# A hybrid decoder trunk on one core: tables and half gates in the first stage, rotary in place, norm gains in the weights

## The chip, the core and the metric

The kernel runs on one core of a Trainium2 chip. The engines are TensorE (PE in the profile, with its weight loads as PEld), VectorE (DVE), ScalarE (ACT), GpSimd (POOL) and SyncE (SP, which here only issues DMAs). The metric is the device time of one execution in microseconds; the median of several runs counts.

## The reference

Two layers run on a sequence of 1024 tokens with 1024 features. Each layer modulates a normalised input by a condition vector c, projects it once, runs three groups of heads, and projects back:

```python
mod = c_act @ w_mod + b_mod                      # c_act = silu(c)
shift, scale, gate = split(mod, 3)
h = rms_norm(x, pre_gain) * (1 + scale) + shift
aq, ak, av, ag, rq, rk, rv, rg, gq, gk, gv, gg, ga = split(h @ w_in)
a_out = window_attention(rotary(aq), rotary(ak), av, sinks) * silu(ag)
r_out = rms_norm(retention(rotary(rq), rotary(rk), rv)) * silu(rg)
g_out = rms_norm(gla(gq, gk, gv, gates(ga)), gla_norm_gain) * silu(gg)
y = concat(a_out, r_out, g_out) @ w_out
x = x + gate * rms_norm(y, post_gain)
```

The rotary angles are position times frequency, one set of 32 frequencies for attention and one for retention; their sines and cosines are made on the chip and are used by both layers. The gain `gla_norm_gain` has 64 entries per layer, the same for all four heads of the third group.

## The kernel before

**Tiles.** The tokens are 8 tiles of 128, in 4 pairs; features are 8 blocks of 128 (KT = 8). The modulated input of a pair is kept transposed, as a high part in the reduced format that TensorE reads and a low part that is the remainder (`hi`, `lo`). Weights are split the same way. A projection of one tile, `project`, is 24 matmuls: three products (high and high, high and low, low and high) for each of 8 blocks. The helper at L161 records almost every matmul, L176 every transpose, L145 many copies on ACT, L150 most DMAs, so these lines stand for many places in the code.

**Weights.** `load` brings one 256-column unit of w_in or w_out in four pieces of 256 KB. The high part is made by ACT (L473) or DVE (L475), the low part by POOL or DVE (L478). The unit of the third group's gate, gg, has 272 columns: 256 of gate and 16 of the low-rank `ga` (L484, L485).

**Buffers.** Four rings of on-chip buffers matter: t2 (512 columns, 10 of them), t1 (256 columns, 8), the PSUM banks `mm` (3) for projections and `aux` for transposes and small results. `mix_tile` gives two large tiles, which hold x of tiles 2 and 3 first, the zeroed operands of the third group later and mixed rows after that.

**Order of work.** The code records the work in an order; a scheduling layer then lays out each engine's instructions and may set one ahead of others recorded earlier. Long steps are generators (`job`), which yield a due time, and `pump` runs those whose time has come by a clock in the code that adds up a cost for each matmul. The due times stand in the table L (pf3, gz1, tt1 and so on). The assignment of operations to engines stands in the table EN. `issue_after` keeps an instruction behind a given one in that layer. Engines take their instructions in order.

**The first stage.** `mod_first` makes shift and gain of layer 0 in two halves (hh = 0, 1) of 512 columns each. The weight tiles `wm` land in pieces on SP's queue. For each of 8 blocks PE multiplies c_act with the shift columns (one row, `pm`), and DVE accumulates the gain columns in `acc` (L322, L324). After a half, ACT copies the row out, and `finish` turns both into columns with 16 tiny matmuls and three small operations on DVE (L304 to L306). The finish of the first half is placed behind the second block of the second half (FIN = 1). Meanwhile x of tiles 0 and 1 is normalised: ACT squares (L530), DVE and POOL make the factor (L513, L514, L519), DVE scales (L545), and PE transposes. Modulation (L577 on ACT, L579 on DVE), the high part (L583, ACT) and the low part (L566, L587) follow. Tiles 2 and 3 come after the first stage (`soon`), tiles 4 to 7 as jobs of `pre_first`.

**After it.** The gates gg and rg of each pair of tiles are projected (`do_gates`), with `silu2` (L861, L863) on each. For gg, `gla_logits` multiplies the silu with the norm gain `gn5` (L872) and stores it to sgS. The sine tables (`tables`, L411 to L439) run as a job from 70 to 93 us in the profile, next to the gates of later tiles, and `tables_T` transposes them. Then the decays of the third group (L918 to L943) and the retention queries rq, with `rotary` (L698 to L704), which reads PSUM three times per tile; each tile of rq holds one of the three `mm` buffers until its third read.

**Small loads.** Constants, the sinks, `gwt` and `gn5` are loaded on SP's queue. The retention gate is stored to srS and loaded again later; those loads are on ACT's queue, other loads on SP's.

Of the kernel before, what the change touches and what calls it, by code (L numbers as in the profile page):

```python
# [89 lines left out]
def trunk(ctx: ExitStack, tc: tile.TileContext, ins, cst, out):  # L90
# [168 lines left out]

    modc = {}  # L260
# [28 lines left out]
    def mod_first(rws, between):  # L289
# [6 lines left out]
        def finish(hh, row, acc):  # L296
            pc = mm()
# [11 lines left out]
        late = None  # L309
        for hh in range(2):  # L310
# [9 lines left out]
            for k in range(KT):  # L320
                if k == 0:
                    V.tensor_scalar(acc, wm[1][:, k], c_act[:, k:k + 1], None, ALU.mult)  # L322
                else:
                    mark[2] = V.scalar_tensor_tensor(acc, wm[1][:, k], c_act[:, k:k + 1], acc, ALU.mult, ALU.add)  # L324
# [3 lines left out]
                if late is not None and k == FIN:  # L328
                    pump()
                    finish(0, *late)  # L330
                    pump()
# [5 lines left out]
        pump()  # L337

    def mod_third(l, j):
# [9 lines left out]
        for hh in range(2):  # L349
            c0 = j * D + 512 * hh  # L350
            acc = gp.tile([P, 512], F32, tag="acc", name=nm("acc"), bufs=1)
            if j == 2:
                G.memset(acc, 0.0)
                nc.sync.dma_start(acc[0:1, :], b_mod[l:l + 1, c0:c0 + 512])
# [44 lines left out]

    MAGIC = 1.5 * 2.0 ** 23  # L400
# [7 lines left out]
    def tables():  # L408
        PIF = float(np.nextafter(np.float32(math.pi), np.float32(0)))
        ang = t2()  # L410
# [3 lines left out]
        nn = t2()  # L414
# [7 lines left out]
        n2 = t2()  # L422
# [4 lines left out]
        red = t2()  # L427
# [4 lines left out]
        yield  # L432
# [5 lines left out]
        yield  # L438
        V.tensor_scalar(cs, cs, 1.0, None, ALU.add)  # L439
# [17 lines left out]

    def unit(l, name):
        return place(PLACE[l][name])

    def load(l, name, first=None):
# [6 lines left out]
        for kc in range(KT // 2):  # L468
# [3 lines left out]
            if first == 0:  # L472
                A.activation(hi, st, AF.Copy)  # L473
            elif first == 1:
                V.tensor_copy(hi, st)  # L475
            else:
                copy(f"whi{kc}", hi, st)
            (G if first == 0 else eng(f"wlo{kc}")).tensor_tensor(wt[:, 1, 2 * kc:2 * kc + 2, 0:256], st, f(hi), ALU.subtract)  # L478
# [32 lines left out]
    def rstd_of(ss, w, scale, eps):  # L511
        r = small(w)
        V.tensor_scalar(r, ss, scale, eps, ALU.mult, ALU.add)  # L513
        G.tensor_tensor(r, r, mhalf[:, :w], ALU.pow)  # L514
# [9 lines left out]
    mark = [None] * 4  # L524
    eb = []

    def squares(xt, to):
        ss = small(2)
        for j in range(2):
            A.activation(to[j], xt[j], AF.Square, accum_out=ss[:, j:j + 1])  # L530
        return ss

    def pre(l, t, xt, early=False, soon=False):
# [7 lines left out]
        for j in range(2):  # L541
            if EN[f"xn{j}"] == "A":
                A.activation(xn[j], xt[j], AF.Copy, scale=r)
            else:
                V.tensor_scalar(xn[j], xt[j], r, None, ALU.mult)  # L545
        yield 0.5 if early else L["pf1"] if soon else lat("pre1", l)


        at = {}

        def turn(kt, bank, i):
            at[kt] = bank[:, i * P:(i + 1) * P]
            transp(at[kt], xn[kt // 4][:, kt % 4 * P:(kt % 4 + 1) * P], ident)

        if early:
            if not eb:
                eb.extend((aux(), aux()))
            x = aux()
            for kt in range(KT):
                turn(kt, x if kt < 4 else eb[kt // 6], kt if kt < 4 else 2 * t + kt % 2)  # L560
        late = []
        for j in range(2):
            yield (0.0, ("modh", l, j))
            if late:
                with tc.issue_after(mark[2].ins):
                    V.tensor_tensor(*late.pop(), ALU.subtract)  # L566
            if not early:
                x = aux()
                for k in range(4):
                    turn(4 * j + k, x, k)  # L570
            hf = t2()
            for k in range(4):
                kt = 4 * j + k
                ks = slice(k * P, (k + 1) * P)
                gain, shift = modc[(l, 1)][:, kt:kt + 1], modc[(l, 0)][:, kt:kt + 1]
                if kt < 6 if early else EN[f"mod{j}"] == "A":
                    A.activation(hf[:, ks], at[kt], AF.Identity, scale=gain, bias=shift)  # L577
                else:
                    mark[3] = V.tensor_scalar(hf[:, ks], at[kt], gain, shift, ALU.mult, ALU.add)  # L579
# [3 lines left out]
            mark[0] = A.activation(hi, hv, AF.Copy)  # L583
            if early and j == 0:
                late.append((lo, hv, f(hi)))
            else:
                i = (V if early else eng(f"hlo{j}")).tensor_tensor(lo, hv, f(hi), ALU.subtract)  # L587
                if early:
                    mark[1] = i
# [5 lines left out]

    def pre_first(t):
# [4 lines left out]

    def mix_tile(dt=F32R):
        return gp.tile([P, 2, KT, P], dt, tag="mx", name=nm("mx"), bufs=2)
# [10 lines left out]

    def between(hh, k):
        if hh == 0 and k == -1:
            load(0, "gg", 0)
        elif hh == 0 and k == 3:
            for t in range(2):
                job(pre(0, t, xe[t], True))  # L620
            pump()
        elif hh == 0 and k == 5:
            clk[0] += 0.6
            pump()
        elif hh == 1 and k == -1:
            for t in (2, 3):
                load_x(t, xe[t], nc.sync)

# [4 lines left out]
    with tc.issue_after(mark[0].ins), tc.issue_after(mark[3].ins):  # L633
        for t in (2, 3):
            job(pre(0, t, xe[t], soon=True))
        pump()
    with tc.issue_after(mark[0].ins), tc.issue_after(mark[1].ins):
        load(0, "rg", 1)
    for t in range(4, NT):
# [719 lines left out]
```

## Time and profile before

| | us |
|---|---|
| Median of 3 runs | 1026.69 (1024.07 to 1027.69) |
| The profiled execution | 1029.65 |
| Its span, first to last instruction | 1027.9 |
| TensorE busy | 989.8 (96%) |
| VectorE, ScalarE, GpSimd busy | 652.7, 388.3, 282.3 |
| Mean granted TensorE clock | 0.981 |
| HBM traffic | 137.1 MB, 133 GB/s over the span |

The profiled execution is one of the fast kind and 2.96 us above the median. Busy times are sums over the whole span; a stage that matters little in them can still set the end. A row of the timeline has the start, the duration, engine and line, what is written and read, the number of instructions merged into it and, in brackets, how long the engine had stood idle before and what released it.

### The profile page before, as it was taken

To read this page: it belongs to the slowest core of one execution; us is meant where nothing else is said; L and a number is where in the kernel's file an instruction comes from. 1 tells how busy PE (TensorE), PEld (TensorE's weight loads), DVE (VectorE), ACT (ScalarE), POOL (GpSimd) and SP (SyncE) were. 2 spreads that over 40 slices of the span, in tenths; PEclk is the share of its full clock that TensorE was granted. 3 is DMA by queue.
4 is the path that set the end of the run, shared out by engine and by line. 5 is a ranking of instruction groups with operands and counts; after the bars stand their busy time and mean duration, and the time that the engine had idled before them with its cause. 6 is when DMAs were issued, how large, how long until landed. Compare 5 with 4: busy or idle time off the path is not lost.

```text
span 1027.9 us, 19498 instructions
## 1 busy us (share of the span) xinstructions
PE 989.8 (96%) x7185; PEld 844.1 (82%) x7185; DVE 652.7 (63%) x1583; ACT 388.3 (38%) x1112; POOL 282.3 (27%) x310
## 2 busy tenths in 40 slices
PE   6899999899999999999999999999999999999997
PEld 2699899889898777777889999988899877777886
DVE  3789756857557687664578296585676477663322
ACT  2476221323222555642554242123332256553111
POOL 2332100424231244431235020133233134532000
PEclk8899999999899999999999999999999999999999
DMA  9742513523225344677545151243132323436753
GB/s 327 270 132 68 170 52 93 162 78 105 91 78 175 93 130 138 220 245 239 180 148 181 47 153 59 84 115 116 35 102 78 113 81 100 135 118 200 230 186 142
DMA packets 124411, 140.46 MB, mean 137 GB/s; under 512 B 12718, under 2 KB 95640, under 8 KB 124316
## 3 DMA queue, kind: packets, MB, share of 16 engines
q1 hardware_dynamic: 116316, 127.50, 40.1%
q10 hardware_dynamic: 8000, 11.72, 3.2%
q8 instruction: 56, 0.92, 0.4%
q14 instruction: 39, 0.32, 0.1%
HBM read 102.48 MB, written 34.60 MB: 133 GB/s over the span
## 4 chain that ended last, share of the span: by engine, by line
PE 77%; DVE 10%; issue 2%; DMA 2%; ACT 2%; POOL 2%; DVEq 0%; POOLq 0%; SPq 0%; ACTq 0%
PE mm L161 59%; PE aux L161 14%; PE aux L176 4%; DMA st<-in_w_mod_dram 2%; DVE arena L478 2%; POOL sm L514 1%; DVE acc L361 1%; ACT t L577 1%; DVE t L930 0%; DVE t L863 0%; DVE arena L587 0%; DVE t L579 0%; DVE t L420 0%; ACT arena L583 0%; DVE arena L147 0%
## 5 line engine op out<-in xcount | busy, mean ns | idle before, releaser
L161 PE MATMUL mm<-arena,arena 128*128 128x256 f32 (+2 forms) x1824 | 305.1, 321 | 3.4 <-DVE t L863 2.6
L161 PE MATMUL mm<-arena 128*128 128x256 f32 (+2 forms) x1824 | 300.2, 319 | 6.3 <-DVE t L701 2.7
L161 PEld LDWEIGHTS mm<-arena,arena 128*128 128x128 f32 x1824 | 257.5, 192 | 29.0 <-issue 4.4
L161 PEld LDWEIGHTS mm<-arena 128*128 128x128 f32 x1824 | 256.8, 193 | 29.3 <-issue 4.4
L161 PE MATMUL mm<-arena,mx 128*128 128x512 f32 (+1 forms) x816 | 184.4, 384 | 0.0
L161 PEld LDWEIGHTS mm<-arena,mx 128*128 128x128 f32 x816 | 145.7, 188 | 33.7 <-issue 1.9
L514 POOL TENSOR_TENSOR sm<-sm,mhalf 128x1 f32<-128x1 f32 (+1 forms) x64 | 53.1, 830 | 324.2 <-DVE sm L513 290.8
L478 POOL TENSOR_TENSOR arena<-st,arena 128x512 fp32r<-128x512 f32 x66 | 96.5, 1470 | 106.3 <-ACT arena L145 77.2
L145 ACT ACTIVATE t<-aux 128x256 f32<-128x256 f32 (+2 forms) x112 | 52.1, 471 | 97.1 <-PE aux L176 63.4
L805 POOL TENSOR_TENSOR smx<-smx,sm 128x512 f32<-128x512 f32 x32 | 36.3, 1135 | 138.5 <-DVE sm L804 119.5
L801 ACT ACTIVATE smx<-smx,sm 128x129 f32<-128x129 f32 x128 | 49.9, 392 | 45.1 <-DVE sm L798 42.4
L145 ACT ACTIVATE arena<-st 128x512 fp32r<-128x512 f32 x90 | 53.4, 624 | 32.9 <-PE mm L161 15.3
L361 DVE SCALAR_TENSOR_TENSOR acc<-st,c_act,acc 128x512 f32<-128x512 f32 x60 | 48.1, 801 | 23.5 <-DMA st<-in_w_mod_dram 23.2
L478 DVE TENSOR_TENSOR arena<-st,arena 128x512 fp32r<-128x512 f32 x62 | 61.4, 1004 | 2.0 <-PE mm L161 0.6
L176 PE MATMUL aux<-c_ident,t 128*128 128x128 f32 x288 | 49.6, 292 | 7.9 <-DVE t L545 5.0
L1119 DVE SCALAR_TENSOR_TENSOR t<-t,sm,t 128x512 f32<-128x512 f32 x32 | 27.0, 877 | 39.9 <-DMA t<-xs 20.3
L1084 DVE TENSOR_TENSOR t<-mm,modg 128x512 f32<-128x512 f32 x30 | 20.7, 689 | 47.7 <-ACT t L1083 47.6
L176 PEld LDWEIGHTS aux<-c_ident,t 128*128 128x128 f32 x288 | 36.0, 148 | 14.7 <-DVE t L545 6.6
L1083 ACT ACTIVATE t<-mm 128x512 f32<-128x512 f32 x30 | 17.9, 596 | 74.8 <-DVE t L1119 36.4
L161 PEld LDWEIGHTS aux<-t,mx 32*128 32x128 f32 (+1 forms) x896 | 41.3, 194 | 4.9 <-issue 2.8
L844 ACT ACTIVATE t<-aux 128x256 f32<-128x256 f32 x32 | 12.3, 383 | 82.9 <-PE aux L161 65.4
L161 PE MATMUL aux<-t,mx 32*128 32x32 f32 (+1 forms) x896 | 42.7, 279 | 0.7 <-DVE t L849 0.5
(191 smaller groups left out, 1250.5 us busy)
## 6 DMA issues: line engine op xcount, KB each, us to landing
st<-in_w_in_dram SPq DMA_DIRECT2D x96, 256.0 KB
st<-in_w_mod_dram SPq DMA_DIRECT2D x64, 256.0 KB
mx<-mixS SPq DMA_DIRECT2D x32, 512.0 KB
mixS<-t SPq DMA_DIRECT2D x64, 128.0 KB
st<-in_w_out_dram SPq DMA_DIRECT2D x32, 256.0 KB
mixS<-t SPq DMA_DIRECT2D x32, 256.0 KB
wm<-in_w_mod_dram SPq DMA_DIRECT2D x12, 512.0 KB
t<-in_x_dram SPq DMA_DIRECT2D x24, 256.0 KB
```

The source lines that it names most:

```text
L145: A.activation(dst, src, AF.Copy)
L161: T.matmul(dst, lhsT, rhs, start=start, stop=stop)
L176: T.transpose(dst, src, idn)
L361: V.scalar_tensor_tensor(acc, wt, c_act[:, k:k + 1], acc, ALU.mult, ALU.add)
L478: (G if first == 0 else eng(f"wlo{kc}")).tensor_tensor(wt[:, 1, 2 * kc:2 * kc + 2, 0:256], st, f(hi), ALU.subtract)
L514: G.tensor_tensor(r, r, mhalf[:, :w], ALU.pow)
L801: A.activation(sm[:, h, :], sm[:, h, :], AF.Exp, bias=mx[:, h:h + 1], accum_out=sums[:, h:h + 1])
L805: eng("pn").tensor_tensor(sm[:, :, 0:128], sm[:, :, 0:128], rs.unsqueeze(2).to_broadcast((P, 4, P)), ALU.mult)
L844: A.activation(sq, po, AF.Square)
L1083: A.activation(yg, pm, AF.Square, accum_out=ss[:, nh:nh + 1])
L1084: V.tensor_tensor(yg, pm, modg[l][:, 512 * nh:512 * nh + 512], ALU.mult)
L1119: V.scalar_tensor_tensor(xt[j], yg[j], r, xt[j], ALU.mult, ALU.add)
```

## The change

- The sine tables move into the first stage. `tables` works in one of the two large tiles instead of four t2 buffers, and its steps are placed by TSTEP between the accumulates: four ahead of the first, four after the fourth, the others after the eighth of the first half. The last steps (two Sin on ACT and two operations on DVE) are recorded when `table_job` is due, with nothing that holds them back; in the built program they stand in the first stage too, on ACT ahead of the first modulations and on DVE on both sides of the second half's first accumulate (the first of the two ahead of it).
- The modulation of tiles 0 and 1 is written out by hand in place of the jobs: norms (`early_norm`), transposes (`early_turn`), the first four blocks behind the first finish, the last four behind the second, half of these on ACT and half on DVE (`early_part`). `finish` uses an `aux` bank instead of `mm`.
- When the first four blocks of tiles 0 and 1 exist, half of each gate gg's projection is recorded (`half_gates`, 12 of 24 matmuls for each tile), one ahead of the second finish and one behind it. `do_gates` records the other half later.
- Squares and norms of tiles 2 and 3 are recorded before the second finish. The loads of x for tiles 4 to 7 stand ahead of most constants in SP's queue, and the due times of their jobs are earlier (pf3 from 13.2 to 9.5).
- `rotary` writes to its destination at once and needs one temporary of its own (`tr`) instead of two t1 buffers. The ring of t1 has 7 buffers instead of 8.
- The gain `gn5` is gone from `gla_logits`. A column `gnc` scales the last 256 rows of w_out in `load`: high parts in ACT's copy or in the product of DVE.
- Loads from srS move from ACT's queue to SP's. The zeroing of the large tiles and of an accumulator on POOL is kept behind a later instruction. Other due times change with it.

The diff, cut to its core:

```diff
@@ mod_first
-            pc = mm()
+            pc = aux()
...
+                if hh == 1 and k == FIN:
+                    finish(0, *first_half)
+                    between(0, KT + 1)
...
             A.activation(row, pm[0:1, :], AF.Copy)
+            between(hh, KT)
             if hh == 0:
-                late = (row, acc)
-        finish(1, row, acc)
-        pump()
+                first_half = row, acc
+            else:
+                finish(hh, row, acc)
+                between(hh, KT + 1)
@@ tables
-        ang = t2()
+        tb = mix_tile(F32).rearrange("p a k q -> p (a k q)")
+        ang = tb[:, 0:512]
...
         V.tensor_scalar(red, red, PIF, -PIF, ALU.min, ALU.max)
-        yield
+        while tail:
+            yield
...
         A.activation(cs, rv, AF.Sin, scale=0.5)
         A.activation(sn, rv, AF.Sin)
         V.scalar_tensor_tensor(cs, cs, -2.0, cs, ALU.mult, ALU.mult)
-        yield
-        V.tensor_scalar(cs, cs, 1.0, None, ALU.add)
+        late["T"] = V.tensor_scalar(cs, cs, 1.0, None, ALU.add)
+
+    def table_steps(n):
+        with tc.issue_after(mark[2].ins) if mark[2] else ExitStack():
+            for _ in range(n):
+                next(tabs, None)
@@ load
+            if name[0] == "o" and kc > 1:
+                if kc == 2:
+                    G.tensor_tensor(wt[:, 1, 4:6, 0:256], st, f(hi), ALU.subtract)
+                else:
+                    V.scalar_tensor_tensor(wt[:, 1, 6:8, 0:256], st, gnc[:, l:l + 1], f(hi), ALU.mult, ALU.subtract)
+                continue
@@ the first stage
+    def half_gates(t):
+        pg0[t] = mm()
+        project(pg0[t][:, 0:272], 0, t, unit(0, "gg"), 272, range(4))
+
     def between(hh, k):
+        if k == -1 or 0 <= k < KT:
+            table_steps(TSTEP[hh][k])
...
+        elif hh == 0 and k == KT:
+            early_turn()
+        elif hh == 0 and k == KT + 1:
+            for t in range(2):
+                mark[0], l_ = early_part(t, 0, 4, "A")
+                lows.append(l_)
...
+        elif hh == 1 and k in HALF:
+            t = HALF.index(k)
+            with tc.issue_after(mark[2].ins):
+                V.tensor_tensor(*lows[t], ALU.subtract)
+        elif hh == 1 and k == KT:
+            half_gates(0)
+            for t in (2, 3):
+                second.append(pre(0, t, xe[t], 2))
+                next(second[-1])
+        elif hh == 1 and k == KT + 1:
+            half_gates(1)
+            for t in range(2):
+                with tc.issue_after(mark[0].ins):
+                    mark[0], la_ = early_part(t, 4, 2, "A")
+                lv = early_part(t, 6, 2, "V")[1]
+                V.tensor_tensor(*lv, ALU.subtract)
+                mark[1] = V.tensor_tensor(*la_, ALU.subtract)
...
@@ small loads
+    for r in range(2):
+        nc.sync.dma_start(gnc[64 * r:64 * r + 64], gn_in.rearrange("l k -> k l"))
+    with tc.issue_after(mark[3].ins):
+        V.tensor_scalar(gnc, gnc, 0.5, None, ALU.mult)
...
@@ rotary
-        a = t1()
-        b = t1()
-        a4 = a[:, 0:nh * 64].rearrange("p (h c k) -> p h c k", h=nh, c=2)
+        b = gp.tile([P, 256], F32, tag="tr", name=nm("tr"), bufs=1)
...
-        V.tensor_tensor(a4, s4, cs.unsqueeze(1).unsqueeze(1).to_broadcast((P, nh, 2, 32)), ALU.mult)
+        V.tensor_tensor(d4, s4, cs.unsqueeze(1).unsqueeze(1).to_broadcast((P, nh, 2, 32)), ALU.mult)
@@ gla_logits
-        sg = silu2(pg)
-        so = t1()
-        eng("gso").tensor_tensor(h4(so), h4(sg), gn5[:, l].unsqueeze(1).to_broadcast((P, 4, 64)), ALU.mult)
-        dma("ssg", sgS[t], so)
+        dma("ssg", sgS[t], silu2(pg))
@@ tables of engines, due times and sizes
-B2, B1, BS, BST, MMB, SMB = 10, 8, 11, 5, 3, 3
+B2, B1, BS, BST, MMB, SMB = 10, 7, 11, 5, 3, 3
...
+HALF = (3, 5)
 FIN = 1
+TSTEP = ((0, 0, 0, 4, 0, 0, 0, 7, 4), (0, 0, 0, 0, 0, 0, 0, 0, 0))
```

In the table EN, `lsr` goes from "A" to "S". In the table L, tb1 goes from 24.5 to 38.9, tt1 from 8.0 to 11.92, pf2 from 4.16 to 4.58, pre1 from 7.44 to 6.55, gz1 from 11.18 to 6.54 and gz2 from 14.05 to 11.24; pf6 (2.1) and pf7 (7.0) are new.

More of the change, by code (lines that the diff above doesn't have):

```diff
@@ L455, in tables_T @@
             nc.sync.dma_start(tabS[p], tb.rearrange("p (s n) -> p s n", s=2))
+    gnc = cp.tile([P, DEPTH], F32, name="gnc")
     def unit(l, name):
@@ L594, in load_x, with later @@
             eng_.dma_start(xt[j], x_in[0, t * P:(t + 1) * P, 512 * j:512 * j + 512])
+    def later(d, gen):
+        yield d
+        yield from gen
     def pre_first(t):
@@ L632, in trunk @@
     arenas.append(ap.tile([P, 4 * SLOT], F32R, name="arena1"))
[L633 to L636, printed above, removed]
     with tc.issue_after(mark[0].ins), tc.issue_after(mark[1].ins):
         load(0, "rg", 1)
+    with tc.issue_after(mark[0].ins), tc.issue_after(mark[1].ins):
+        for t in range(2):
+            job(later(L[f"pf{6 + t}"], second[t]))
+        pump()
+    mark[3] = mark[1]
     for t in range(4, NT):
@@ L665, in gla_tiles @@
             z_ = mix_tile(F32).rearrange("p a k q -> p (a k q)")
[L666 removed]
+            with behind("G"):
+                G.memset(z_, 0.0)
             if b == 0:
@@ L1141, in do_gates @@
             for t in (2 * p, 2 * p + 1):
-                pg = mm()
+                half = l == 0 and name == "gg" and t in pg0
+                pg = pg0[t] if half else mm()
                 if name == "gg":
-                    project(pg[:, 0:272], l, t, w, 272)
+                    project(pg[:, 0:272], l, t, w, 272, range(4 if half else 0, KT))
                     job(gla_logits(l, t, pg[:, 0:256], pg[:, 256:272]))
```

167 lines of the change are left out of this document (86 added, 81 removed).

## The prediction

> **What bounds the kernel now.** I read the page first: busy times, slices, chain of waits.
>
> ```profile
> span 1027.9 us, 19498 instructions
> ...
> PE 989.8 (96%) x7185; PEld 844.1 (82%) x7185; DVE 652.7 (63%) x1583; ACT 388.3 (38%) x1112; POOL 282.3 (27%) x310
> ...
> PEclk8899999999899999999999999999999999999999
> ...
> PE 77%; DVE 10%; issue 2%; DMA 2%; ACT 2%; POOL 2%; DVEq 0%; POOLq 0%; SPq 0%; ACTq 0%
> ```
>
> TensorE (PE) is busy 96% of the span: 1027.9 - 989.8 = 38.1 us idle is nearly all an edit that removes no matmul can win, with what half-clock stretches cost. The change removes no matmul, so the question is how much of the 38.1 lies where it works. The windows by stage (columns: PE, PE weight load, DVE, ACT, POOL busy; clock; DMA share; GB/s) answer that:
>
> ```profile
> 20.00:30.00 10.00, 10.00 (x36) 4.50 (x37) 4.89 (x7) 2.63 (x6) 7.21 (x6) 0.81 1.07 369
> 30.00:40.00 10.00, 7.00 (x32) 3.70 (x31) 8.10 (x20) 7.23 (x18) 0.53 (x1) 0.87 1.02 341
> 40.00:50.00 10.00, 8.79 (x56) 8.56 (x56) 6.92 (x19) 3.43 (x12) 5.57 (x5) 0.78 0.56 184
> 50.00:60.00 10.00, 8.33 (x67) 7.94 (x66) 8.64 (x23) 7.89 (x22) 4.79 (x5) 1.00 0.47 137
> 60.00:70.00 10.00, 10.00 (x86) 9.95 (x85) 8.53 (x19) 6.80 (x22) 3.44 (x4) 1.00 0.64 191
> ...
> 80.00:90.00 10.00, 9.41 (x77) 9.19 (x76) 10.00 (x24) 5.46 (x12) 1.29 (x1) 1.00 0.08 26
> ...
> 110.00:120.00 10.00, 8.29 (x57) 8.32 (x58) 10.00 (x36) 2.80 (x7) 0.00 (x0) 0.83 0.37 108
> ```
>
> Until 40 us DMA is full (1.02 to 1.07): weights set the pace, and DVE has room (4.89 of 10 in 20 to 30). From 30 to 60 PE lacks 5.88 us and twice runs below full clock. From 60 to 110 it is nearly full, while DVE is loaded to 8 or 10. At 110 PE stands again with DVE at 10.00. So the change has a DMA-bound hole to put work into, and two places to win: 30 to 60, and 110.
>
> The timeline of PE (start, duration, line; in brackets idle before it and its releaser) names the holes:
>
> ```profile
> 34.83 1.05 PE L161 MATMUL mm<-c_ones,t 128*128 128x1 f32 x8 [1.20 <-DVE t L324]
> ...
> 36.79 0.77 PE L161 MATMUL mm<-arena 128*128 128x272 f32 x4
> 39.37 6.75 PE L161 MATMUL mm<-arena 128*128 128x272 f32 x34 [1.80 <-ACT arena L583]
> ...
> 48.19 1.09 PE L176 MATMUL aux<-c_ident,t 128*128 128x128 f32 x8 [1.21 <-DVE t L545]
> ...
> 58.20 2.05 PE L161 MATMUL mm<-arena 128*128 128x272 f32 x14 [1.63 <-DVE sm L513]
> ...
> 111.71 4.58 PE L161 MATMUL mm<-arena 128*128 128x256 f32 x24 [2.25 <-DVE t L701]
> ```
>
> The 272-column rows also show the clock: 34 matmuls in 6.75 us, 0.198 each, against 24 in 3.27 us (0.136) at 89.53, with the clock granted at full. The 24 of 256 columns at 111.71 took 4.58, where 48 took 6.00 at 79.93 (0.125 each, 3.0 for 24).
>
> **The accounts.** The profiled execution took 1029.65 us (span 1027.9 plus 1.75 around it), 2.96 above the median of 1026.69. I sum against 1029.65 and take off 2.96. About 0.3%, 3.1 us, can be told from no change.
>
> **Part 1: half gates and norms ahead.** Before, PE needs 21.41 us from the end of the second finish (36.79) to the first gate matmul of tile 2 (58.20). That is 48 of 272 columns (48 x 0.136 = 6.5), 48 of 256 (6.1), 16 transposes (rows of 1.03 and 1.09 for 8, 2.1), idle 1.80 + 1.21 + 1.63 = 4.64, and half clock: 34 x (0.198 - 0.136) = 2.1. Sum 21.4.
>
> After, 24 of the 48 gate matmuls need only the first half's shift and gain. In PE's new order tile 0's 12 stand before finish(1), tile 1's 12 behind it; the first 12 (1.6) fill the wait of 1.20, the others the 1.80 in which ACT and DVE make the second half. That half is now shared: per tile two modulations and a cast on each of ACT and DVE, some 2.2 us from the second gain (0.4 behind the finish) for tile 0, less 1.64 of cover: about 0.8 remains. Squares and norms of tiles 2 and 3 now precede finish(1), so the 1.21 before tile 3's transposes goes, and tile 2's 1.63 if its two halves are ready.
>
> With T for when the accumulation on DVE (new L331) ends: finish 2.03 (the two rows from 34.83 to 36.86), half gates 1.64, 0.8, 24 x 0.136 = 3.3, transposes 2.1, 48 matmuls 6.1. Tile 2 starts at T + 16.0 at full clock. Before, T was 34.83. An unmoved T gives 50.8, 7.4 earlier than 58.20. T will move.
>
> **Part 2: the tables in the head.** The tables' 19 or so DVE operations (0.42 to 0.69 us each at 70 to 93 us; about 11.6 in all, one stretched to 1.78) now lie before 33 us. Four stand ahead of the first accumulate: PE's first matmul moves from 6.4 to about 7.7, covered by the weights (4.0 us of DVE idle on wm). Six follow the first half's last accumulate at about 21: 3.7 us. Then ACT loads its table (1.28 measured) and makes two Sin (0.63 and 0.61); the operation that needs the Sin (new L451) stands on DVE ahead of the second half's first accumulate and of the first half's shift and gain (new L312 to L314). Behind those wait ACT's modulations and PE's half gates. DVE alone: 21.0 + 3.7 + 0.3 (gate weights) + 0.9 to the first Sin + 0.7 + 8 accumulates (6.0) and two subtractions (1.4) = 34.0; the last weights land at about 33.1, which leaves two accumulates behind them, 34.6. With a little blocking T is 35.8, and first shift and gain come at 28.5 (before: 30.18).
>
> DVE is not alone. POOL makes the gate weights' low parts in the same stretch, and the timelines of DVE and POOL show what that did before:
>
> ```profile
> 26.09 1.28 DVE L485 TENSOR_TENSOR arena<-t,arena 128x128 fp32r<-128x128 f32 x1 [5.11 <-ACT arena L484]
> 27.29 1.96 DVE L322 TENSOR_SCALAR t<-wm,c_act 128x512 f32<-128x512 f32 x1
> ...
> 25.94 1.28 POOL L478 TENSOR_TENSOR arena<-st,arena 128x512 fp32r<-128x512 f32 x1 [1.32 <-ACT arena L473]
> 27.15 1.81 POOL L666 MEMSET mx<- 128x2048 f32 x1
> ```
>
> L485 costs 0.28 without POOL's operation beside it, L322 0.49; here each lasted until POOL's ended. In the new order POOL has four such (1.25 each) while DVE has six table operations; alternating, four pairs take 4 x 1.94 = 7.8, the other two 1.4, so the tables end near 30 rather than 25. First shift and gain then come at about 32.5 and T at 38.8. The MEMSETs have left the head. Bounds for T: 35.8 and 38.8; I take 37, since POOL starts its four only as ACT's casts arrive and some fall into DVE's waits. Tile 2 then starts at 53.0.
>
> The Trainium skill, "SBUF — State Buffer", "Who interferes with whom", speaks against this placement: GpSimd shares a port pair with DVE under an exclusive lock, and the later one is blocked, not slowed. The rows agree. By that rule alone T would be 38.8.
>
> Against 58.20 that is 5.2. I take off 1.2: tile 2's low parts now wait on DVE behind the new gain column gnc (new L726) and the sink copies, whose small DMAs stand on SP behind tile 7's loads, which wait for tile 2's transposes (about 42). Ten issues at the 0.47 spacing of the rows at 47 to 50 us put them at 46.5, landing around 49 to 52, and the tile is wanted at 53: zero to 1.7, near the lower end. Tile 4's norms may cost 0 to 1.5 more. **Head: 4.0, bounds 1.7 and 6.4.** The upper one is T = 35.8 without the 1.2; the lower one T = 38.8, 3.4, less 1.7 because PE idle of over 3 us before T brings half clock back.
>
> **Part 3: around 110 us.** PE waited 2.25 there for the rotary, then ran 24 matmuls in 4.58 instead of 3.0: 3.8 in all. DVE loses the 11.6 of tables, 3.4 of gain products in the gates (8 x 0.42, L872) and the sink copies. But the row before the rotary is a chain of decays (L918 to L939, 107.23 to 110.68), released by the last logits and still ahead of the first rotary in the new order, and PE arrives 4 earlier. Bounds 0 and 3.8; **2.0**, about the middle.
>
> **Part 4: edits with one answer.** Rotary in place: the same five operations, two t1 buffers fewer in use, one buffer "tr" that is always waited for in order on DVE itself: 0. Gain folded into w_out's weights: DVE gets two 0.75 operations for one 0.69 and two on POOL swap places, once per load, while PE is full and 3.4 of DVE per layer go: 0. Layer 1's hole of 1.98 at 555 us (on DVE L863, behind which L872 stood) may shrink by 0.5. Table loads on ACT: the same number, moved. Loads of srS on SP instead of ACT: 0.33 each, hidden by a PE that is full; the rival below prices the uncovered case.
>
> Sum: 1029.65 - 4.0 - 2.0 = 1023.65; less 2.96, **1020.7, forecast 1020.5**.
>
> **Rivals.** *Port contention eats the head* (0.18): T is 38.8, the head yields 1.7, the rest 2.0: 1023.0, up to 1025 if the hole at 110 stays too. For it: the two rows above. Against: DVE idled 5.11 before L485.
>
> *The hole at 110 stays* (0.12): the decays bind, not DVE's backlog; the head's 4.0 alone: 1022.7. For it: L918 follows 1.4 us after the logits' last operation. Against: DVE is at 10.00 there.
>
> *The SP queue makes it slower* (0.15): SP issues in order, and the row "SPq L150 <- ACT t L145" of its waits has 150.1 us in 42 waits, 17.6 the longest. Sixteen loads of srS now stand in that queue, with seven t1 buffers instead of eight; a load held by a buffer also holds mix and weight loads behind it. At the mean wait, 3.6, all sixteen exposed would cost 57; slower by 3.1 needs 6 + 3.1 = 9.1, that is 0.57 exposed per load. Then 1030 to 1036. Against it: from 115 us on PE idles only 11.4 in holes over 0.3, none of them on these loads.
>
> *The clock* belongs to the bounds: if PE's idle before T stays under 2 us, no half-clock window follows, else 1.7 comes back. The Trainium skill, "TensorE: Matmul & The Clock Gate", Part 1, says an idle window of about 3.4 us halves the clock; by it, T = 37 keeps full clock, as in my sum. The trace shows halving also where idle was 2.25, at 111.71, which the rule alone would not give.
>
> **Chances.** Forecast case 0.55 (1014 to 1023.5, all faster). Of the contention rival 0.10 is faster, 0.08 the same; of the hole's 0.07 and 0.05; the queue rival's 0.15 is slower. Faster 0.72, same 0.13, slower 0.15. Best ends: 6.4 + 3.8 and 0.5 for layer 1 give 1016.0, widened to 1013.5 for holes beyond; the range to 1028.5 takes in both mild rivals and leaves out the queue.
>
> **What would show it.** Right: idle before the second finish under 1 us in spite of a later T; half gates in front of and behind it; tile 2's gates near 53; clock 0.9 or more from 30 to 50; less than 1 us idle at the first rotary. Wrong: L442 beside POOL at over 1.2 us each; first shift and gain after 32; DVE idle on gnc; PE holes past 120 us whose releaser is a load of srS; any slower total.

## The result and the profile after

| kernel | median us | runs | ratio to before |
|---|---|---|---|
| before | 1025.45 (1020.31 to 1030.22) | 20 | 1 |
| the change | 1029.13 (1022.76 to 1035.52) | 20 | 1.0037, 95% interval 1.0020 to 1.0055 |

The change makes the kernel slower by 0.4%, 3.7 us between the medians. The forecast was 1020.5, with a range up to 1028.5. With more runs the kernel before has a median of 1025.45 instead of 1026.69, so its profiled execution, 1029.65, was 4.2 above the typical one. (Ratios here and below are made of undisturbed executions; medians are of all.)

Of the page of the changed kernel, the same lines as before:

```profile
span 1027.0 us, 19464 instructions
...
PE 986.5 (96%) x7185; PEld 840.1 (82%) x7185; DVE 647.4 (63%) x1567; ACT 390.1 (38%) x1116; POOL 280.6 (27%) x310
...
PEclk9899999999899999999999999999999999999999
...
PE 77%; DVE 7%; DMA 3%; issue 3%; ACT 2%; POOL 1%; SPq 0%; DVEq 0%; POOLq 0%; ACTq 0%
```

These lines hardly differ from before; spans of 1027.9 and 1027.0 even look like a gain. One pair of executions can't show 0.4% here. What can is the time at which TensorE (PE) starts its i-th instruction: both kernels have 7185 of them, in nearly the same order. To know which part of the old profile was its own, the kernel before and the change were profiled once more. Start times in us behind the second execution of the kernel before:

| PE instruction | 300 | 700 | 1350 | 1800 | 2250 | last |
|---|---|---|---|---|---|---|
| at, before again | 73.3 | 124.8 | 208.0 | 252.5 | 291.2 | 1014.7 |
| before, first profile | -2.3 | 0.0 | -0.6 | -0.8 | +4.6 | +6.2 |
| the change | +3.3 | +3.3 | -0.2 | -0.7 | +7.8 | +5.8 |
| the change again | +3.5 | +3.1 | -0.3 | -0.7 | +3.9 | +4.2 |

The change is late by 3.3 to 3.5 us at the gates' 300th instruction (5.6 against the first profile, whose head ran 2.3 earlier), wins that back until the 1350th, and loses again between the 1800th and the 2250th, in the third head group's part of layer 0. The first profile of before lost 5.5 in that part too, by half-clock stretches (clock 0.75 from 270 to 290 us) which its second execution does not have (1.00).

The windows of the change (PE, PE weight load, DVE, ACT, POOL, clock, DMA share, GB/s):

```profile
20.00:30.00 10.00, 7.45 (x33) 3.38 (x32) 9.41 (x11) 3.65 (x6) 6.74 (x6) 0.83 1.08 362
30.00:40.00 10.00, 6.69 (x26) 2.73 (x25) 8.27 (x19) 8.12 (x21) 0.24 (x1) 1.00 1.07 375
40.00:50.00 10.00, 8.86 (x46) 8.61 (x46) 7.38 (x20) 6.26 (x13) 3.58 (x4) 0.66 0.25 87
50.00:60.00 10.00, 8.88 (x75) 8.63 (x73) 3.60 (x11) 3.07 (x9) 1.27 (x1) 1.00 0.39 103
60.00:70.00 10.00, 7.13 (x52) 6.60 (x52) 8.31 (x16) 6.83 (x18) 4.29 (x4) 1.00 0.75 219
...
110.00:120.00 10.00, 8.35 (x72) 8.15 (x71) 9.96 (x33) 1.64 (x3) 0.00 (x0) 1.00 0.60 171
```

DVE went from 4.89 to 9.41 of 10 in 20 to 30: the hole is filled. But DVE is then nearly idle (3.60) from 50 to 60, and PE falls to 7.13 from 60 to 70, where it was full. PE's timeline names the new holes:

```profile
39.57 1.33 PE L161 MATMUL aux<-c_ones,t 128*128 128x1 f32 x8 [2.33 <-DVE sm L549]
40.83 1.86 PE L161 MATMUL aux<-c_ones,row 1*128 1x1 f32 x8
42.62 5.95 PE L161 MATMUL mm<-arena 128*128 128x272 f32 x30
...
61.48 0.64 PE L161 MATMUL mm<-arena 128*128 128x272 f32 x3 [2.60 <-ACT arena L632]
...
65.78 1.27 PE L161 MATMUL mm<-arena 128*128 128x272 f32 x8 [0.91 <-ACT arena L632]
...
112.97 0.66 PE L176 MATMUL aux<-c_ident,t 128*128 128x128 f32 x4 [1.65 <-DVE t L467]
```

The second finish starts at 39.57 instead of 34.83 and runs in part at half clock (3.1 us instead of 2.03), as do the 30 gate matmuls behind it (0.198 each). Tile 2's gates stop for 2.60 us behind their first four. The old hole at 111.71 is gone, but a new one of 1.65 stands there: transposes of the tables, which wait for a copy on DVE. What DVE and POOL did in the head, and what DVE waited for ahead of tile 2:

```profile
23.18 1.50 DVE L438 TENSOR_SCALAR mx<-mx 128x512 f32<-128x512 f32 x1
24.71 4.04 DVE L442 SCALAR_TENSOR_TENSOR mx<-mx 128x512 f32<-128x512 f32 x3
...
30.71 0.69 DVE L451 SCALAR_TENSOR_TENSOR sincos<-sincos 128x512 f32<-128x512 f32 x1 [0.70 <-ACT sincos L449]
...
57.98 0.17 DVE L726 TENSOR_SCALAR gnc<-gnc 128x2 f32<-128x2 f32 x1 [2.60 <-DMA gnc<-in_gla_norm_gain_dram]
59.00 0.49 DVE L756 COPY sink<-sm 128x8 f32<-128x8 f32 x2 [0.85 <-DMA sm<-in_attn_sinks_dram]
59.40 1.35 DVE L564 TENSOR_SCALAR t<-aux,mod,mod 128x128 f32<-128x128 f32 x4
...
23.14 4.33 POOL L508 TENSOR_TENSOR arena<-st,arena 128x512 fp32r<-128x512 f32 x3
```

L438, 0.42 us by itself, lasts 1.50; two of the three L442 last 1.64 instead of 0.69, while POOL's low parts run (23.14 to 27.47). Behind the tables DVE waits another 0.70 for a Sin of ACT (L451). And the half of tile 2's modulation that stands on DVE could start at 56.2, when the second group of eight transposes ends; it starts at 59.40, behind two waits for small loads. (Tile 2's own transposes are the group of 49.95 to 50.98. By the order of the code the second group, from 55.17, is tile 3's, and it frees the t2 buffers that tile 2's modulation writes.)

### The profile page after: what moved, and what is told of

The parts are those of the page before. It is cut to its first block, busy times and chain, and to the rows that moved or that the text cites. A ratio compares the mean times of both kernels' runs of the same rounds, so it can differ in the third digit from the quotient of the medians.

```text
span 1027.0 us, 19464 instructions
## 1 busy us (share of the span) xinstructions
PE 986.5 (96%) x7185; PEld 840.1 (82%) x7185; DVE 647.4 (63%) x1567; ACT 390.1 (38%) x1116; POOL 280.6 (27%) x310
## 4 chain that ended last, share of the span: by engine, by line
PE 77%; DVE 7%; DMA 3%; issue 3%; ACT 2%; POOL 1%; SPq 0%; DVEq 0%; POOLq 0%; ACTq 0%
PE mm L161 60%; PE aux L161 14%; PE aux L176 4%; DMA st<-in_w_mod_dram 2%; DVE arena L508 1%; POOL sm L544 1%; DMA st<-in_w_in_dram 1%; DVE acc L370 1%; DVE t L776 0%; ACT arena L145 0%; DVE arena L147 0%; DMA mixS<-t 0%; DVE t L771 0%; DVE t L923 0%; POOL arena L508 0%
## 5 line engine op out<-in xcount | busy, mean ns | idle before, releaser
L161 PEld LDWEIGHTS mm<-arena 128*128 128x128 f32 x1824 | 255.2, 191 | 30.2 <-ACT arena L632 4.0
L508 POOL TENSOR_TENSOR arena<-st,arena 128x512 fp32r<-128x512 f32 x58 | 83.1, 1443 | 101.5 <-ACT arena L145 71.7
L145 ACT ACTIVATE arena<-st 128x512 fp32r<-128x512 f32 x82 | 49.0, 626 | 48.3 <-DMA st<-in_w_in_dram 19.0
L508 DVE TENSOR_TENSOR arena<-st,arena 128x512 fp32r<-128x512 f32 x54 | 53.9, 1013 | 3.4 <-ACT arena L145 1.4
L176 PE MATMUL aux<-c_ident,t 128*128 128x128 f32 x288 | 46.8, 280 | 5.5 <-DVE t L574 2.1
L1153 ACT ACTIVATE t<-mm 128x512 f32<-128x512 f32 x30 | 17.9, 595 | 73.7 <-DVE t L1189 38.5
L176 PEld LDWEIGHTS aux<-c_ident,t 128*128 128x128 f32 x288 | 33.9, 142 | 11.2 <-DVE t L574 2.3
```

What stands on the lines that cost most here:

```text
L145: A.activation(dst, src, AF.Copy)
L161: T.matmul(dst, lhsT, rhs, start=start, stop=stop)
L176: T.transpose(dst, src, idn)
L1153: A.activation(yg, pm, AF.Square, accum_out=ss[:, nh:nh + 1])
```

## The experiments

All are single edits or sums of edits of the changed kernel, as short diffs. Ratios are to the kernel before, with 95% intervals.

| run | median us | ratio |
|---|---|---|
| e1, small loads early | 1023.46 | 1.0000 (0.9973 to 1.0028) |
| e2, e1 and Sin behind the squares | 1021.83 | 0.9995 (0.9966 to 1.0024) |
| e3, e1 and low parts on DVE | 1021.63 | 0.9953 (0.9925 to 0.9980) |
| e5, all three | 1022.44 | 0.9948 (0.9921 to 0.9975) |
| e4, tables back | 1027.96 | 1.0022 (0.9994 to 1.0050) |
| e8, tables back, loads early | 1024.58 | 0.9991 (0.9969 to 1.0012) |
| e7, e5 without half gates | 1028.55 | 1.0047 (1.0019 to 1.0075) |
| e13, the change with eight t1 buffers | 1022.97 | 0.9974 (0.9948 to 1.0000) |
| e11, e5 with eight t1 buffers | 1019.44 | 0.9940 (0.9916 to 0.9965) |
| e10, e11 and srS loads on ACT | 1017.32 | 0.9918 (0.9887 to 0.9949) |
| e14, e10 and low parts behind T | 1016.20 | 0.9909 (0.9874 to 0.9943) |

In the traces: T is the end of the second half's last accumulate, G the end of the first half's shift and gain, F the end of the first finish on PE, "300th" the start of PE's 300th instruction.

| run | F | G | T | 300th |
|---|---|---|---|---|
| before, two profiles | 28.4, 30.8 | 30.2, 32.5 | 34.8, 37.1 | 71.0, 73.3 |
| the change, two profiles | 29.0, 29.0 | 32.7, 32.8 | 39.4, 39.5 | 76.6, 76.8 |
| e1 | 31.2 | 32.4 | 39.1 | 72.4 |
| e2 | 30.3 | 32.3 | 39.0 | 69.0 |
| e3 | 30.1 | 30.5 | 37.4 | 68.5 |
| e5 | 28.9 | 30.3 | 37.0 | 67.6 |
| e4 | 30.8 | 31.8 | 38.5 | 74.4 |
| e8 | 28.5 | 29.5 | 36.2 | 67.3 |
| e10 | 28.1 | 29.6 | 36.3 | 68.3 |
| e14 | 28.1 | 29.6 | 35.3 | 68.6 |

**The kernels again.** Expected of the kernel before:

> The kernel before, unchanged, profiled a second time, to see which of its holes and half-clock stretches are its own and which belong to one execution. If the loss at the first gates of layer 1 (a hole of 1.98 us at 555 and half clock behind it) is its own, it shows again at 548 to 556 us; the hole of 2.25 at 111.7 as well, within 0.5. If the profiled execution of 1029.65 us was only a slow one, the second takes 1023 to 1028 and its holes at 555 or at 268 to 294 differ.

It took 1023.40. The hole of 1.98 us at the first gates of layer 1 is its own (2.02 at 549.9), that at 111.7 partly (1.48), the half clock at 268 to 297 and at 556 is not. F, G and T all came 2.4 later with the weights.

Expected of the change:

> The changed kernel, unchanged, profiled a second time. DVE idle for gnc ahead of tile 2's modulation 2 to 3 us again, T (end of the second half's last accumulate) at 39 to 40, the table operations beside POOL's at over 1.2 us each, the 300th TensorE instruction at 75 to 78. If these were one execution's, they differ by more than 1.5.

1027.24, and all as expected: T 39.48, L442 at 1.64 twice, 300th at 76.8. In the kernel before, the weights' landing moves T. In the change DVE sets it: from the end of the first half's last accumulate (23.3) to T it takes 16.2 us in both profiles, and in e13, which leaves the head as it is, F came earlier (28.6) and T did not (39.65).

**Small loads (e1).**

```diff
@@ between(1, -1): behind load_x of tiles 2 and 3
+    for r in range(2):
+        nc.sync.dma_start(gnc[64 * r:64 * r + 64], gn_in.rearrange("l k -> k l"))
+    nc.sync.dma_start(sinkn, sinks.rearrange("(o a) b -> o (a b)", o=1).to_broadcast((P, 16)))
```

> Edit: the two gnc loads and the sinks load stand on SP ahead of the x loads of tiles 4 to 7, behind x of tiles 2 and 3; nothing else. Theory A (two separate costs: the accumulation in the head ends late, T = 39.4 us, and DVE waits 2.60 + 0.85 us on small loads ahead of tile 2's modulation): T stays near 39.4, the hole of 2.60 at tile 2's gates (61.48 us) shrinks below 0.6, the 300th TensorE instruction starts at 72.5 to 74 instead of 76.6; time 1025 to 1027. Rival B (the small loads are the whole loss): 71 or earlier, 1023. Rival C (the holes of tiles 3 to 5 come from DVE and ACT being overloaded anyway): the hole moves to tile 3, 300th at 76, time 1029.

Theory A held: T stays (39.1), the hole at tile 2 is gone, the 300th starts 4.1 us earlier than in the change. DVE's timeline of e1 has no wait there any more:

```profile
50.41 0.15 DVE L732 TENSOR_SCALAR gnc<-gnc 128x2 f32<-128x2 f32 x1
50.48 0.23 DVE L760 COPY sink<-sinkn 128x8 f32<-128x8 f32 x2
```

So the wait of 2.60 and 0.85 us has grown by the time that the tiles behind it are through. From tile 2's fourth gate matmul (the 199th instruction) to the 300th the change needs 18.0 us and e1 13.0; e1 had come to the 199th 0.8 later, which leaves the 4.1. E4 and e8 below differ by the same edit and need the same 18.0 and 13.0.

**Tables back (e4, e8).** The tables run from 78 to 100 us again, on four t2 buffers; e8 has the small loads early too.

> Edit: the sine tables go back to where they were (a job from about 70 us on, four t2 buffers), all the rest as changed. Theory A: T returns to 35 us, first shift and gain come at about 28, the second finish ends near 37; the wait for gnc stays, since its loads follow tile 2's transposes, but earlier (landing near 53); 300th TensorE instruction at 71 to 73; the hole before rk/rq near 110 us is back in part (1 to 3 us); time 1026 to 1029. Rival B (small loads alone): T earlier but the 300th stays within 2 us of 76.6. Rival D (DVE was late for another reason than tables): T over 38.

> Edit: both of the two edits above: tables back at their old place, small loads early. Theory A: the costs add; T 35, no hole over 1 us at tile 2's gates, 300th TensorE instruction at 66 to 68.5 (before: 71.0), so half gates and early norms alone bring 3 to 5 us of the head; the hole near 110 us returns (2 to 4); time 1021 to 1025. Rival C (holes of tiles 3 to 5 remain whatever comes before): 300th at 70 to 72, 1025 to 1027.

In e8 G follows F by 1.0 us and T is 36.2; the change has 3.7 between F and G. The 300th comes at 67.3. In the first profile of the kernel before, where the weights landed alike (F 28.4), it is 71.0: half gates and early norms bring 3.7 there, as theory A had it. In e4 the small loads still hold tile 2 (a hole of 2.63 at 59.4) and take most of it back. My number for e4's T, 35, was wrong: the weights landed late (F 30.8), and even with F at 28.5, in e8, T is 36.2. At 107 to 114 us both have a hole of 2.1.

**Port or Sin (e2, e3, e5).**

```diff
@@ e2: first half of the tables' tail, then its DVE part
+            with tc.issue_after(late["A"].ins):          # behind the squares of tiles 2 and 3
+                tail.clear()
+                next(tabs, None)
...
+            with tc.issue_after(mark[1].ins):            # behind tile 1's low parts
+                next(tabs, None)
@@ e3
-            (G if first == 0 else eng(f"wlo{kc}")).tensor_tensor(...)
+            (V if first == 0 else eng(f"wlo{kc}")).tensor_tensor(...)
```

> Small loads early, and the Sin with its table load moved behind the squares on ACT, its two DVE operations behind tile 1's low parts; POOL still makes the gate weights' low parts. It stands between e1 (neither mended) and e5 (both). If the wait for the Sin is what holds first shift and gain: they come 1.1 to 1.8 us earlier than in e1 (32.3), near 30.8, T near 37.6. If the port lock is: they stay within 0.7 of e1.

> Small loads early, and the gate weights' four low parts on DVE instead of POOL; the Sin and its two DVE operations stay where the change put them. If the port lock is what costs: no table operation lasts over 0.8 us and first shift and gain come at 29.5 to 30.8 (limited by the second half's first weights and the first finish), T near 37; DVE has 2.8 us more work of its own. If the lock cost no more than that work: 32, T 39.

> Edit: tables stay in the head, but the gate weights' low parts go from POOL to DVE (no POOL operation beside the tables), the two Sin with their table load come behind the squares of tiles 2 and 3 on ACT and the two DVE operations behind tile 1's low parts, and the small loads are early. Theory A: table operations take their own 0.42 to 0.69 us each, first shift and gain at about 30, T 36 to 37, no wait on gnc; 300th TensorE instruction at 67 to 70; the hole near 110 stays closed; time 1020 to 1024. Rival C: 300th at 72 to 74, 1025 to 1027. Rival E (port contention cost little; DVE's own work fills the head): T over 38.

Read by the clock time alone, taking the Sin out of the way moves G by nothing (32.3 against 32.4 in e1). But DVE came later to the tables in e2: the first half's last accumulate ended at 24.2, in e1 at 22.9. From that end to G it is 9.5 us in both profiles of the change, in e1 and in e13, 8.1 in e2, and 6.8 in e3, e5, e10 and e14 (6.8 and 7.5 in e7 and e11, where G follows F by 0.4 and so waits for PE). So both cost something: the wait for the Sin 1.4, and POOL's four low parts another 1.3, though DVE then has them to do itself. E3 has both savings with one edit, since the scheduling layer now set the operation that needs the Sin (L451) behind the first shift and gain (L312 to L314). G is then 30.5, 0.4 behind F. DVE in e3:

```profile
23.64 1.89 DVE L508 TENSOR_TENSOR arena<-st,arena 128x512 fp32r<-128x512 f32 x3
...
25.65 0.42 DVE L438 TENSOR_SCALAR mx<-mx 128x512 f32<-128x512 f32 x1
26.10 2.15 DVE L442 SCALAR_TENSOR_TENSOR mx<-mx 128x512 f32<-128x512 f32 x3
...
29.82 0.42 DVE L444 TENSOR_SCALAR mx<-mx 128x512 f32<-128x512 f32 x1
30.16 0.15 DVE L312 TENSOR_TENSOR sm<-aux,sm 128x4 f32<-128x4 f32 x1
...
30.93 0.69 DVE L451 SCALAR_TENSOR_TENSOR sincos<-sincos 128x512 f32<-128x512 f32 x1 [0.42 <-ACT sincos L449]
```

Four low parts cost DVE 0.63 each here; on POOL they took 1.27 and up, and held DVE's operations for as long. So POOL's share is the shared port, not DVE's own work. The Trainium skill, "SBUF — State Buffer", "Who interferes with whom", has this rule of an exclusive lock, and here the rule alone would have given the better T: 38.8, where I took 37.

That e2 reaches the 300th 3.5 us before e1 with the same T is not explained by G or T: e1 has a hole of 2.06 and a half-clock stretch at 49 us that e2 has not. In the hole PE waits for a low part (L704) that stands on DVE behind a norm of 1.51; in e2 the scheduling layer laid the two out the other way round. The hole (1.1 to 2.1) is in every trace that has half gates and not e2's edit (the change, e1, e3, e4, e8, e13) and in none that has the edit, so it goes with the edit's order. The half clock does not: e3 has the same hole (2.05) and full clock behind it. E5's profiled execution took 1034.36, 12 more than its median; only its head is read.

**Half gates (e7).** E5 without the two calls of `half_gates`.

> The head mended as in e5 (seven t1 buffers), but no half gates: each gate's 24 matmuls of tiles 0 and 1 stand together again behind the second finish. By the prediction's Part 1 the half gates fill 1.2 to 3 us of PE's waits: the 200th to 300th TensorE instructions come 2 to 3 us later than in e5, time 1.5 to 3 us longer than e5. Rival: PE's wait is then covered by other work, difference under 0.7.

Slower than e5 by 1.0% (1.0047 against 0.9948), more than expected. At the 200th instruction it is 4.2 us behind e5 (58.6 against 54.4), which is the half gates' own, with the half clock that e7 has from 39 to 48 us (0.50) and e5 has not (1.00); another 3.7 come at 62 us, where the new order makes PE wait for a later tile's norm:

```profile
65.56 1.97 PE L176 MATMUL aux<-c_ident,t 128*128 128x128 f32 x8 [3.26 <-DVE t L619]
```

So half gates bring some 4 us, and due times laid out for them don't suit a kernel without.

**The ring (e13, e11).**

```diff
-B2, B1, BS, BST, MMB, SMB = 10, 7, 11, 5, 3, 3
+B2, B1, BS, BST, MMB, SMB = 10, 8, 11, 5, 3, 3
@@ rotary
-        b = gp.tile([P, 256], F32, tag="tr", name=nm("tr"), bufs=1)
+        b = t1()
```

> The changed kernel with one edit: the t1 ring has eight buffers again, and rotary takes its temporary from it (there is no room for eight and tr). Theory F (one t1 buffer fewer makes ACT wait at 257 to 262 us for a store of the mix to finish): ACT's wait of 5.46 us ahead of the square at 261.4 falls below 2, the hole of 2.22 at 262.7 below 0.8, so that from the 1800th to the 2000th TensorE instruction it loses under 1 us against the kernel before instead of 3.7; time 1024.5 to 1027. Rival G (that stage is late because its due times or the queue of stores changed): the hole stays over 1.5, time as the change.

> Low parts of the gate weights on DVE, Sin behind the squares, small loads early (all three of the head's mends), and eight t1 buffers with rotary's temporary from them. If the head's costs and the ring's are separate they add: 300th TensorE instruction 5 to 6 us before that of the kernel before in a like execution, no loss over 1 us from the 1800th to the 2000th; time 1017 to 1021, ratio to before 0.992 to 0.996. If the ring costs nothing: as e5, 0.995.

The second profile of the change has, on ACT and on PE, the first two lines; e13 the last two, at the same step:

```profile
261.42 0.38 ACT L917 ACTIVATE t<-aux 128x256 f32<-128x256 f32 x1 [5.46 <-DMA mixS<-t]
262.74 0.67 PE L161 MATMUL aux<-stG,t 128*128 128x256 f32 x2 [2.22 <-DVE sm L543]
```

```profile
259.03 0.39 ACT L917 ACTIVATE t<-aux 128x256 f32<-128x256 f32 x1 [1.85 <-DMA mixS<-t]
...
260.75 0.59 PE L161 MATMUL aux<-stG,t 128*128 128x256 f32 x2
```

ACT's square writes a t1 buffer, and the profile puts its wait down to a store of the mix (in e1 and e2 to a load, so which transfer it is stays uncertain). With seven buffers the square comes at 261.42, though PE's matmuls ahead of it were done at 258.7 (in the kernel before it came at 258.22); DVE's reduction waits for it, and behind that in DVE's queue stands the state that PE needs. With eight the hole is gone. From the 1800th to the 2250th instruction the change again lost 4.6 us against the kernel before, e13 won 0.6. E13 is level with the kernel before or ahead of it (0.9974, interval to 1.0000), with an unchanged, late head (300th at 77.1). The edit lets the scheduling layer lay out another order too, so it is the ring with its order that is measured.

The hole itself follows the ring in every trace: with seven buffers ACT idles 4.9 to 6.0 us ahead of that square and PE 1.7 to 2.8 us at that step (nine traces), with eight ACT idles 1.7 to 1.9 and PE has no hole there (four traces). In time the gains do not add. The head's mends (e5, 0.9948) and e13's gain of 0.0063 would make 0.9885; e11 is 0.9940 (0.9916 to 0.9965) and can't be told from e5; its 300th instruction came 4.2 us before that of the second profile of before, where 5 to 6 were expected. Between the 1350th and the 2250th instruction e11 loses 5.2 us against the kernel before, as e2 (4.9) and e3 (5.1) do with seven buffers. One reason is a new hole of 2.03 at 245.9: PE waits for DVE's masked copy (L1072), which stands behind an accumulate that waits for a load of w_mod. E14 has this hole too (2.04), e13 a smaller one (0.63), e10 none.

**SP's queue (e10) and the low parts (e14).**

```diff
@@ e10: e11 and
-"lsr": "S"
+"lsr": "A"
@@ e14: e10 and
-HALF = (3, 5)
+HALF = (7, 7)
...
-            half_gates(0)      # ahead of the second finish
...
+            half_gates(0)      # behind it, ahead of half_gates(1)
```

> As e11, but the sixteen loads from srS stand on ACT's queue again as before the change. The prediction's SP rival (a load held in SP's queue holds the others): 1 to 4 us faster than e11. My reading (no hole past 120 us has a load of srS as its releaser): within 1 us of e11.

E10 is 0.9918, e11 0.9940 (2.1 us between the medians), and the intervals overlap: whether the srS loads cost anything on SP is not settled. No hole of PE in any trace has such a load as its releaser.

> As e10 (head mended, eight t1 buffers, srS loads on ACT), but the two low parts of the first half stand behind the last accumulate instead of between the accumulates, and both tiles' half gates behind the second finish. If those two subtractions, which wait for ACT's high parts, are what makes the stretch from first gain to T 6.8 us instead of 4.6: it falls to 4.5 to 5.2, T to about 34 to 35.5 by the weights' landing, and tile 2's gates start 0.5 to 2 us earlier than in e10; time 0 to 2 us shorter. Rival: weights bind T, the stretch stays over 6 and the time is the same or, since no half gate covers the wait before the second finish any more, up to 2 us longer.

From G to T it is now 5.7 us instead of 6.7; the weights end the last accumulate. Tile 2's gates start at 54.13 instead of 54.24. So the two low parts between the accumulates make 1.0 of the 2.1 us by which G to T is longer than in the kernel before, and moving them wins nothing that can be measured (0.9909 against 0.9918): the half gate that covered the wait has moved as well. E14 and e10 are the fastest kernels here, 0.8 to 0.9% ahead of the one before.

## Why the prediction was wrong

The likeliest case (faster by 6) was wrong in sign. Three terms of the sum failed: T (taken 37, measured 39.4), the small loads (taken 1.2, measured 4.9 between the 199th and the 300th instruction), and the smaller ring of t1 (taken 0, measured 5.2 in one stage). Point by point, against the first profile of before, by which it was made:

- **Part 1, the sum T + 16.0.** The sum's own terms hold, at full clock. In the change tile 2's gates start at 58.19 = 39.4 + 18.8. The 2.8 more are the finish at half clock (1.1) and the 30 gate matmuls behind it (30 x 0.062 = 1.9), less 0.2 elsewhere. I had taken full clock, with T at 37; a later T left PE idle for 2.33 us ahead of the finish, and half clock followed.
- **Part 2, T.** Taken 37, between 35.8 and 38.8; it came at 39.4, 2.4 later and beyond the upper bound. The reason given for the middle, that POOL's operations would fall into DVE's waits, failed: L438 and two L442 lasted as long as POOL's. G came at 32.7, and 32.5 was worked out for the alternating case, but that agreement is partly luck: the first half's last accumulate ended at 23.3 and not at 21.0, and from there to G it took 9.5 us and not 11.5, of which 1.4 are the wait for the Sin. The rest is G to T: 6.7 us where the sum had 6.3.
- **The small loads.** The step said 1.2, of 0 to 1.7, by issues at 46.5 and a landing at 49 to 52. The mechanism is the one named (gnc behind tile 7's x on SP, those behind tile 2's transposes); its size failed by the start from which it was worked out. The transposes of tile 2 were put at about 42, and the prediction's own terms give 44 even for T = 37 (37 + 2.03 + 0.8 and 31 gate matmuls of 0.136, which stand ahead of them). T came later and the clock was half: the transposes came at 49.95 to 50.98, SP issued gnc at 54.75, and DVE had it at 57.98. What the forecast left at nothing is what follows: holes of 0.91, 0.48 and 0.76 at the next tiles. By e1 and e8 all of it is 4.9. So one late thing moved another: a cost of the change that hangs on another cost should be priced at that one's bad end. The lower bound of the head took T = 38.8 and half clock, and left the small loads out.
- **The head together.** Forecast -4.0, bounds -6.4 and -1.7. Tile 2's gates start where they did (58.19 against 58.20), and what the holes behind them cost makes it +5.6 at the 300th instruction (+3.3 to +3.5 against the second profile of before). With both costs mended (e3, e5) it is -2.5 and -3.4: the order does what it is meant to.
- **Part 3, the hole at 110.** Forecast -2.0. From the 300th to the 700th instruction the change wins 2.3 against the first profile of before, and 0.0 and 0.4 against its second, where the hole was 1.48 without half clock. The new hole of 1.65 at the tables' transposes, not foreseen, takes what goes with the old one. Moving the tables does win there against the same kernels with the tables back: 3.7 us (the change against e4) and 2.5 (e1 against e8).
- **Part 4, edits "with one answer".** The step that priced rotary in place and its buffers at 0 is the third that failed. It looked at rotary's own use of t1 and not at who else takes from the ring. With the late head, seven buffers cost 5.2 us from the 1800th to the 2250th instruction (4.6 against -0.6) and the difference between 1.0037 and 0.9974 in all; with the mended head no gain of eight is shown (e11 against e5).
- **The clock.** The condition was no half clock if PE's idle ahead of T stays under 2 us. The change idled 2.33 there, and the half clock came. But e10 idled 0.64 and had it too (last section), so the condition is not enough.
- **The rivals.** Port contention was right as a mechanism, and too small as a price. The slower rival (SP's queue with seven t1 buffers) had the buffers in it, but as what holds a load; the ring held ACT, and no load of srS. So the chance that it gave to a slower kernel was right for another reason.
- **Not foreseen, and not explained:** between the 700th and the 1350th instruction the change wins 3.4 to 3.5 us. E4, e8, e10 and e13 have it too (2.8 to 4.3 against the second profile of before), so it is neither the tables, nor the ring, nor the srS loads; rotary in place, the missing gain product and the due times were not tried apart. And e10, e11 and e14 lose 3, 5 and 3 us of their lead between the 1350th and the 2250th. The hole behind L1072 explains 2 of it in e11 and e14; the rest is open.

## What to carry to other kernels

Count every user of a buffer ring before taking one buffer away: the engine that pays may be one whose line was not touched, in another stage, through a transfer that is still under way. Measure a mend in the kernel that it is meant for: two that pay apart need not add. Compare a wait from the event that starts it, not by clock time, when the weights' landing differs between executions. Before filling an engine's hole with moved work, look at what its port neighbour does in that hole, and put the two on one engine if they collide. A wait that hangs on another forecast time is priced at that time's late end; and a stage that was the weights' to set can become the engine's, after which early weights help no more.

## What the hardware showed that I had not expected

- The weights' landing in the first 30 us moves by over 2 us between executions of one kernel (F at 28.4 and 30.8 in the kernel before), and the hole at 110 us takes the difference up.
- Half clock does not follow visible idle time alone. In e10 PE was busy 2.72 and 2.58 of 3 us from 33 to 39 and had 0.50 of the clock from 42 to 45, so that 19 gate matmuls took 4.67 us; in e3 it was busy 2.37 and 1.43 of 3 from 42 to 48 and kept full clock:

```profile
42.00:45.00 3.00, 3.00 (x15) 3.00 (x15) 3.00 (x7) 2.98 (x7) 1.84 (x2) 0.50 0.46 176
```

```profile
45.00:48.00 3.00, 1.43 (x12) 1.43 (x13) 3.00 (x5) 1.23 (x2) 1.23 (x1) 1.00 0.04 14
```

The first line is e10's, the second e3's. Ahead of the half clock e10 ran the 16 matmuls of one column in `finish` (36.42 to 38.42). E3 ran them too (37.58 to 39.58), so they alone do not explain it; the cause is open. Such stretches make single profiles of one kernel differ by 5 us (the two of the kernel before between the 1800th and 2250th instruction), more than this change moved its median.
